# A hybrid decoder step: the first stage's loads, norm row, page table and key copies rearranged, decays stored by chunks

## The chip, the cores and the metric

The kernel runs on one core of a Trainium2 chip. The core has TensorE (PE: matrix products and transposes into PSUM), VectorE (DVE), ScalarE (ACT), GpSimd (POOL) and SyncE (SP, which here issues nearly all DMA transfers). Each engine takes its own instructions strictly in order and waits on semaphores for the others; the transfers of all queues share 16 DMA engines. The metric is the device time of one execution in microseconds (us), the median of several runs.

## The reference

One decoder layer is applied to 512 prompt tokens with 16 learned meta tokens in front, and to 64 sample tokens (8 sequences of 8). Shapes: width 1024, 32 state-space heads of 64 with state 128, 16 attention heads over 4 key/value heads, 8 indexer heads of 64.

```python
u = rmsnorm(h, norm1_w)                      # x * rsqrt(mean(x^2)+eps) * w
z, xbc, dt_raw, q, k, v, qi, ki, wi, g_ssm, g_attn = split_in(u @ w_in)
# state-space branch: causal conv + silu on xbc, then per chunk of 128 tokens
acum  = cumsum(softplus(dt_raw + dt_bias) * -exp(a_log))
decay = exp(where(causal, acum[i] - acum[j], -inf))
y     = (cb * decay) @ (x * dt) + (cc @ h) * exp(acum)
# attention branch: indexer scores choose the keys (128 of the prompt, 256 of a sample's)
s   = sum_h relu(qi . ki) * wi               # sample keys: cache_kidx[page_table]
att = softmax(q . k[top], ...) @ v[top]
# merge, then MLP
h = h + (sigmoid(g_ssm) * (y @ w_ssm_proj) + sigmoid(g_attn) * (att @ w_attn_proj)) @ w_out
h = h + square(relu(rmsnorm(h, norm2_w) @ w_up)) @ w_down
```

Outputs are the final-normalised tokens, the new key, value and indexer rows, and the new convolution and state-space states.

## The kernel before, in words

All 592 tokens stand as columns. Products that need fp32 accuracy are done as three products of rounded parts: each operand is split into a high part (a rounded copy, made by ScalarE) and a low part (the rest, made by VectorE), and `mm3` (line 145) adds high x high, low x high and high x low over 8 slices of 128 rows, 24 matmuls for one block of 128 output columns and one half of the tokens (288 or 296 columns). `weights` (line 130) loads a 512 KB block through one of two raw buffers `wr`, and splits it into `wh` (line 122) and `wl` (line 123), three buffers each. A half's result lies in one of two PSUM buffers of the tag `w`. Other PSUM results take the tags `a` and `s`, three buffers each, which `mis()` hands out in turn.

**First stage (lines 170 to 235, pool `p0`).** SP loads the first x tile of 128 tokens, the first 532 columns of the constants (`cst`, 266 KB), `norm1_w` read once for every partition (`w1row`, 512 KB), the second and third x tile, the first weight block `w0` (indexer keys, indexer weights, time steps; two transfers), the fourth tile, and a fifth one with the 64 sample and 16 meta tokens. For each of the five tiles ScalarE squares and sums (line 202), VectorE and GpSimd make the reciprocal root (lines 154, 155), VectorE multiplies by it and by the norm row (`xn`, line 205), TensorE transposes eight slices (line 211), ScalarE writes the high part `uh` (line 213) and VectorE the low part `ul` (line 214). `xn` and the squares' scratch share a tag with two buffers. Then come the loads of a second weight block (`wq0`), of the convolution weights, of `ssm_norm_w` and of the convolution state, and their transposes (lines 221 to 234). The first half of a projection needs the first three tiles, the second half all five.

**Indexer stage (lines 288 to 500, pool `p1`).** The pool takes the place of `p0`; it is declared with the default for reused memory, by which its first instructions wait for the whole of the old pool. It loads the other constants (line 290), runs the first projection (`smT`), then the four blocks of indexer queries (`qS`: ScalarE line 321, VectorE line 322), makes the page table's row numbers (lines 330 to 340: one load, seven VectorE operations), and scores the prompt's keys (lines 344 to 360). `idx_unit` (line 379) handles two sample sequences: GpSimd gathers the indexer keys of each (`kr`, two buffers), and they are copied side by side into `kg`:

```python
pool.indirect_dma_start(out=kr, ..., in_offset=bass.IndirectOffsetOnAxis(ap=idx[:, b:b + 1], axis=0))
(act.copy if b2 else pool.tensor_copy)(kg[:, :, b2, :], kr.rearrange("p (s c) -> p s c", s=8))
```

Transposes (line 394) and a product with the sample queries (line 404) follow. Then VectorE picks the top 128 keys of each prompt row (lines 420, 421). The time steps and their sums `acum` are made (lines 426 to 467); their transposed form `acT` (32 heads x 640 tokens) goes to DRAM as `d_ac`, its exponential as `d_ec` (lines 469, 471). Projections for keys, values and queries follow.

**Scan (lines 612 to 816).** Four groups of 8 heads, each with five chunks (four of 128 tokens, one of the 80 others, of which 64 are used here). For each chunk, `chunk` loads the heads' sums spread over the tokens' partitions (`bc`, two loads of four heads, line 719) and the exponentials spread over 64 partitions for each head (`EB`, two loads, line 713). ScalarE turns `bc` into decays (lines 721, 723). Convolution and gate projections are interleaved with it.

After that come gates, sample attention, prompt attention, the merge and the MLP, which the change doesn't touch.

**What sets the order.** The program is written in one order; at build time a planner goes through it with modelled times of its own, and writes each engine's instructions in the order in which they become ready in that model, earlier program lines first. On the chip this order is fixed: an instruction whose input is late holds everything behind it on its engine.

Of the kernel before, what the change touches and what calls it, by code (L numbers as in the profile page):

```python
# [33 lines left out]
def _consts():  # L34
    p = np.arange(128)[:, None]
    j = np.arange(128)[None, :]
    blk = np.where(np.arange(128) < 64, np.arange(128) // 8, np.arange(128) // 16 + 4)
    same = blk[:, None] == blk[None, :]
    v = (p // 64) * 8 + p % 8
    parts = [  # L40
        ("ident", p == j),
        ("tri", j >= p),
        ("tri4", (j >= p) & same),
        ("ones", np.ones((128, 128))),
        ("off8", np.arange(8)[None, :] != 2 * (p // 32) + p % 32 // 8),
        ("half", np.full((128, 8), -0.5)),
        ("in32", np.arange(4)[None, :] == (p % 32) // 8),
        ("blk4", same),
        ("neg", np.where(j > p, NEG, 0.0)),
        ("cneg", np.where(j > p, -BIG, 0.0)),  # L50
        ("sel", np.arange(32)[None, :] == v),
        ("neg8", np.where(np.arange(8)[None, :] > p % 8, NEG, 0.0)),
        ("in8", np.arange(8)[None, :] == p // 8),
        ("pg8", np.arange(8)[None, :] == p // 16),
        ("mod16", p % 16),
        ("odd2", (p % 2) == (j // 64)),
        ("pair16", np.arange(16)[None, :] == p // 2),
    ]
# [12 lines left out]
def body(ctx, tc, a, o):  # L71
# [36 lines left out]
    def flat(t):  # L108
        return t.rearrange("p a b -> p (a b)")
# [63 lines left out]
    p0_stack = ctx.enter_context(ExitStack())  # L173
    p0 = p0_stack.enter_context(tc.tile_pool(name="p0", bufs=1))

# [5 lines left out]

    wrow = p0.tile([128, D], FT, name="w1row")
    xts = []
    for t in range(5):
        xt = p0.tile([128, D], FT, tag="xt", name="xt", bufs=5)
        load_x(t, xt)
        if t == 4:
            sy.dma_start(xt[64:80], meta)
        if t == 2:
            w0 = weights([(lambda r: r[:, :, 0:96], w_in[:, C_KI:C_KI + 96].rearrange("(k p) c -> p k c", p=128)),  # L190
                          (lambda r: r[:, :, 96:128], w_in[:, C_DT:C_DT + 32].rearrange("(k p) c -> p k c", p=128))], lo_eng=dve)
        if t == 0:
            sy.dma_start(cst[0], a["cst"][:, 0:KEPT])
            sy.dma_start(wrow, rows(a["norm1_w"], D))
        xts.append(xt)
    ssq = p0.tile([128, 5], FT, name="ssq1")
    rs = p0.tile([128, 5], FT, name="rs1")
    for t in range(5):
        n = 128 if t < 4 else 80
        xt = xts[t]  # L200
        jk = p0.tile([128, D], FT, tag="jk", name="jk", bufs=2)
        act.activation(jk[:n], xt[:n], AF.Square, accum_out=ssq[:n, t:t + 1])
        rstd_of(rs[:n, t:t + 1], ssq[:n, t:t + 1], D, 1, n)
        xn = p0.tile([128, D], FT, tag="jk", name="xn", bufs=2)
        dve.scalar_tensor_tensor(xn[:n], xt[:n], rs[:n, t:t + 1], wrow[:n], op0=OP.mult, op1=OP.mult)
        for q in range(2):
# [5 lines left out]
            h_ = uh[:, 4 * q:4 * q + 4, 128 * t:128 * t + n]  # L212
            act.activation(h_, pv[:, :, :n], AF.Copy)
            dve.tensor_tensor(ul[:, 4 * q:4 * q + 4, 128 * t:128 * t + n], pv[:, :, :n], h_.bitcast(FT), op=OP.subtract)  # L214
    wq0 = weights([(lambda r: r, block(w_in, 0, C_QI))])

    cwr = p0.tile([128, 128], FT, name="cwr")
    sy.dma_start(cwr[0:96], a["conv_w"][0].rearrange("k (t c) -> (k t) c", c=128))
# [3 lines left out]
    act.activation(cwT, ps[:, :120], AF.Copy, scale=0.5)  # L222
    nwr = p0.tile([16, 128], FT, name="nwr")
# [4 lines left out]
    scr = p0.tile([24, 3072], FT, name="scr")  # L228
    sy.dma_start(scr, a["state_conv"][0].rearrange("b r c -> (b r) c"))
# [18 lines left out]
    d_y = drp.tile([16, 128, NQ], FT, name="d_y")  # L248
    d_ac = drp.tile([32, 640], FT, name="d_ac")
    d_ec = drp.tile([32, 640], FT, name="d_ec")  # L250
    d_xd = drp.tile([16, 128, NT], FT, name="d_xd")
# [35 lines left out]

    with tc.tile_pool(name="p1", bufs=1) as p1:
        cst.append(p1.tile([128, CST.shape[1] - KEPT], FT, name="cst1"))
        sy.dma_start(cst[1], a["cst"][:, KEPT:])  # L290
        sm_tok = p1.tile([128, 5, 128], FT, name="sm_tok")
        smT = p1.tile([128, NT], FT, name="smT")
# [34 lines left out]
        split(kiT[:, 0:528], kS, kL)  # L327


        pt = p1.tile([128, 64], I32, name="pt")  # L330
        ptf = p1.tile([128, 8, 8], FT, name="ptf")
        ptx = p1.tile([128, 8], FT, name="ptx")
        sy.dma_start(pt, rows(a["page_table"], 64))
        dve.tensor_copy(flat(ptf), pt)
        dve.tensor_tensor(ptf, ptf, K("pg8")[:, None, :].to_broadcast([128, 8, 8]), op=OP.mult)
        dve.tensor_reduce(ptx, ptf, axis=AX, op=OP.add)
        dve.tensor_scalar(ptx, ptx, 16.0, K("mod16"), op0=OP.mult, op1=OP.add)
        dve.tensor_copy(idx, ptx)
        for h in range(2):
            dve.tensor_scalar(idx2[:, :, h], ptx, 2.0, float(h), op0=OP.mult, op1=OP.add)  # L340

# [37 lines left out]
        def idx_unit(pr):  # L379
            kiP = p1.tile([128, 1032], FT, tag="kiP", name="kiP", bufs=2)  # L380
            kg = p1.tile([128, 8, 2, 64], FT, tag="kg", name="kg", bufs=2)
            for b2 in range(2):
# [3 lines left out]
                                        in_offset=bass.IndirectOffsetOnAxis(ap=idx[:, b:b + 1], axis=0))  # L386
                (act.copy if b2 else pool.tensor_copy)(kg[:, :, b2, :], kr.rearrange("p (s c) -> p s c", s=8))
            dv = kiP[:, 0:1024].rearrange("c (p s) -> c s p", s=8)
# [36 lines left out]

        brow = p1.tile([128, 2, 32], FT, name="brow")
        sy.dma_start(brow[:, 0, :], rows(a["dt_bias"], 32))
        sy.dma_start(brow[:, 1, :], rows(a["a_log"], 32))
        X = p1.tile([128, 5, 32], FT, name="X")
# [38 lines left out]
        dve.tensor_copy(acT[:, 512:640], ps[:32, 0:128])  # L468
        sy.dma_start(d_ac, acT)
        act.activation(acT, acT, AF.Exp)  # L470
        sy.dma_start(d_ec, acT)
        ps = mis()
# [139 lines left out]
    with tc.tile_pool(name="p3", bufs=1, reuse_waits="tile") as p3, \  # L612
# [88 lines left out]
        def chunk(g, c):  # L701
# [563 lines left out]
```

## Time and profile before

| | |
|---|---|
| median of 3 runs | 1494.07 us (1493.74 to 1494.7) |
| the profiled execution | 1499.61 us, its span 1497.8 us |
| busy share of the span | PE 96%, DVE 65%, ACT 46%, POOL 22% |
| mean granted clock of TensorE | 0.955 |
| DMA | 221.54 MB in 297609 packets |
| sizes of transfers | `w1row` 512 KB, `cst` 266.0 KB and 292.5 KB, `scr` 288.0 KB, x tiles and weight blocks 512 KB, `bc` 256 KB (32 times) and 64 KB (8 times), `EB` 128 KB (32 times) and 64 KB (8 times) |

A row of the timeline has the start in us, the duration, the engine, the line and the operation, its output and inputs with their shapes, how many were merged into the row, and in brackets how long the engine had been idle and what released it. The chain is the work that ended last, followed back from the end of the stretch: each step names what released the next. A wait row reads: who waited for whom, total us, times, longest. In the table by stretches, each engine's busy us stand with the number of its instructions in parentheses, then the granted clock as a share of full speed, the share of the 16 DMA engines, and GB/s. Merged matmuls overlap in the pipeline, so the duration of one is longer than the step to the next.

### The profile page before, as it was taken

To read this page: it belongs to the slowest core of one execution; us is meant where nothing else is said; L and a number is where in the kernel's file an instruction comes from. 1 tells how busy PE (TensorE), PEld (TensorE's weight loads), DVE (VectorE), ACT (ScalarE), POOL (GpSimd) and SP (SyncE) were. 2 spreads that over 40 slices of the span, in tenths; PEclk is the share of its full clock that TensorE was granted. 3 is DMA by queue.
4 is the path that set the end of the run, shared out by engine and by line. 5 is a ranking of instruction groups with operands and counts; after the bars stand their busy time and mean duration, and the time that the engine had idled before them with its cause. 6 is when DMAs were issued, how large, how long until landed. Compare 5 with 4: busy or idle time off the path is not lost.

```text
span 1497.8 us, 26553 instructions
## 1 busy us (share of the span) xinstructions
PE 1443.2 (96%) x9960; PEld 1293.7 (86%) x9960; DVE 973.9 (65%) x2010; ACT 695.1 (46%) x1548; POOL 324.1 (22%) x475
## 2 busy tenths in 40 slices
PE   6899999999999999999999999999999999999998
PEld 5899989987888888889688888898898998899886
DVE  5599989998868767582644777665654444444434
ACT  4454255546665654542655777732352331232211
POOL 1100011426636335342423633100000000000001
PEclk9899999999999999999999999999999999999999
DMA  6334365768897887878964532146143321231202
GB/s 178 107 66 118 115 173 167 208 195 220 231 263 201 255 221 197 247 198 252 293 228 142 155 87 79 43 129 194 50 133 93 99 85 57 85 112 58 84 28 70
DMA packets 297609, 221.54 MB, mean 148 GB/s; under 512 B 43821, under 2 KB 267361, under 8 KB 297457
## 3 DMA queue, kind: packets, MB, share of 16 engines
q1 hardware_dynamic: 292232, 200.98, 47.5%
q0 software_dynamic: 5248, 18.88, 3.7%
q8 instruction: 78, 1.28, 0.4%
q14 instruction: 51, 0.41, 0.1%
HBM read 174.97 MB, written 44.07 MB: 146 GB/s over the span
## 4 chain that ended last, share of the span: by engine, by line
PE 76%; DMA 11%; DVE 5%; ACT 2%; issue 2%; SPq 1%; POOL 1%; POOLq 0%; DVEq 0%; ACTq 0%
PE w L145 22%; PE s L1177 16%; PE a L145 14%; PE w L1039 7%; PE s L871 2%; PE a L1177 2%; PE s L1005 2%; DMA out_dram<-st 1%; DMA bc<-d_ac 1%; DMA wr<-in_w_ssm_proj_dram 1%; DMA st<-in_state_ssm_dram 1%; PE s L734 1%; PE a L894 1%; PE a L995 1%; DMA d_x<-tk 1%
## 5 line engine op out<-in xcount | busy, mean ns | idle before, releaser
L145 PE MATMUL w<-uh,wh 128*128 128x288 f32 (+1 forms) x1168 | 359.1, 307 | 12.8 <-DVE qS L322 4.3
L145 PE MATMUL w<-uh,wl 128*128 128x288 f32 (+1 forms) x1168 | 354.9, 304 | 0.0
L145 PE MATMUL w<-ul,wh 128*128 128x288 f32 (+1 forms) x1168 | 352.6, 302 | 0.6 <-DVE ul L214 0.6
L145 PEld LDWEIGHTS w<-uh,wh 128*128 128x128 f32 x1168 | 223.6, 191 | 20.5 <-issue 7.1
L123 DVE TENSOR_TENSOR wl<-wr,wh 128x1024 fp32r<-128x1024 f32 x129 | 161.1, 1249 | 117.1 <-ACT wh L122 114.9
L145 PEld LDWEIGHTS w<-ul,wh 128*128 128x128 f32 x1168 | 223.5, 191 | 3.9 <-issue 2.3
L145 PEld LDWEIGHTS w<-uh,wl 128*128 128x128 f32 x1168 | 222.4, 190 | 1.5 <-issue 0.8
L122 ACT ACTIVATE wh<-wr 128x1024 fp32r<-128x1024 f32 x129 | 136.3, 1056 | 147.5 <-PE w L145 84.5
L145 PE MATMUL a<-u2h,wh 128*128 128x288 f32 (+2 forms) x512 | 151.4, 296 | 0.0
L145 PE MATMUL a<-u2l,wh 128*128 128x288 f32 (+2 forms) x512 | 151.2, 295 | 0.0
L145 PE MATMUL a<-u2h,wl 128*128 128x288 f32 (+2 forms) x512 | 151.2, 295 | 0.0
L1177 PE MATMUL s<-dl,hh 128*128 128x512 f32 (+1 forms) x324 | 126.9, 392 | 0.0
L1177 PE MATMUL s<-dh,hh 128*128 128x512 f32 (+1 forms) x324 | 126.8, 392 | 0.0
L1179 DVE TENSOR_TENSOR h<-h,s 128x512 f32<-128x512 f32 (+1 forms) x91 | 61.2, 679 | 100.4 <-PE s L1177 100.3
L122 ACT ACTIVATE dh<-wr 128x1024 fp32r<-128x1024 f32 x40 | 42.5, 1062 | 178.1 <-PE s L1177 138.3
L155 POOL TENSOR_TENSOR rs<-rs,cst 128x1 f32<-128x1 f32 (+2 forms) x15 | 8.3, 552 | 446.0 <-DVE rs L154 445.9
L1177 PE MATMUL s<-dh,hl 128*128 128x512 f32 (+1 forms) x260 | 101.7, 391 | 0.0
L145 PEld LDWEIGHTS a<-u2l,wh 128*128 128x128 f32 x512 | 96.1, 188 | 0.6
L145 PEld LDWEIGHTS a<-u2h,wh 128*128 128x128 f32 x512 | 96.1, 188 | 0.6
L145 PEld LDWEIGHTS a<-u2h,wl 128*128 128x128 f32 x512 | 96.1, 188 | 0.0
L1039 PE MATMUL w<-ysh,wh 128*128 128x288 f32 x256 | 78.4, 308 | 0.2 <-DVE ms L1044 0.2
L123 DVE TENSOR_TENSOR dl<-wr,dh 128x1024 fp32r<-128x1024 f32 x40 | 49.0, 1225 | 45.3 <-ACT dh L122 45.2
(384 smaller groups left out, 3220.1 us busy)
## 6 DMA issues: line engine op xcount, KB each, us to landing
wr<-in_w_in_dram SPq DMA_DIRECT2D x64, 512.0 KB
wr<-in_w_up_dram SPq DMA_DIRECT2D x32, 512.0 KB
wr<-in_w_down_dram SPq DMA_DIRECT2D x32, 512.0 KB
st<-in_state_ssm_dram SPq DMA_DIRECT2D x16, 512.0 KB
bc<-d_ac SPq DMA_DIRECT2D x32, 256.0 KB
out_dram<-st SPq DMA_DIRECT2D x16, 512.0 KB
wr<-in_w_ssm_proj_dram SPq DMA_DIRECT2D x16, 512.0 KB
d_xd<-th SPq DMA_DIRECT2D x16, 296.0 KB
```

Of the source, the lines that this page charges most:

```text
L122: act.activation(hi, raw, AF.Copy)
L123: (lo_eng or dve).tensor_tensor(lo, raw, hi.bitcast(FT), op=OP.subtract)
L145: pe.matmul(ps[:, :c1 - c0], p[:, k, :], x[:, c0:c1], start=(k == 0 and i == 0), stop=(k == 7 and i == 2))
L155: pool.tensor_tensor(dst, dst, K("half")[:p, :cols], op=OP.pow)
L734: pe.matmul(py[64 * (hh % 2):64 * (hh % 2) + 64, 128 * (hh // 2):128 * (hh // 2) + n], xt[:n, 64 * hh:64 * hh + 64], mt, start=True, stop= ...
L871: pe.matmul(v[64 * hp:64 * hp + 64], QZ[:, hp, :], kk, start=True, stop=True)
L894: pe.matmul(py[h, 0:128], PTs[:, s, h], Vg[s // 4][:, 256 * (s % 4) + 128 * hp:256 * (s % 4) + 128 * hp + 128], start=(s == 0), stop=False)
L995: pe.transpose(pv[:, j, :], P2[:, e, 128 * j:128 * j + 128], idf)
L1005: pe.matmul(py[64 * e:64 * e + 64, 0:256], Vt[:, j, kv:kv + 64], PT[:, e, j], start=(j == 0), stop=False)
L1039: pe.matmul(ps[:, :HQ], p[:, k, mc], x[k][:, c0:c1], start=(k == 0 and i == 0), stop=(k == 3 and i == 2))
L1177: pe.matmul(ps, x, w[:, cc], start=(k == 0 and i == 0), stop=(k == len(ws) - 1 and i == len(terms) - 1))
L1179: dve.tensor_tensor(h2[:, t, cc], h2[:, t, cc], ps, op=OP.add)
```

## The change

- `norm1_w` is loaded once, as one row of 4 KB, first of all transfers. TensorE spreads it: a column of ones (one row deep, so K = 1) times the row, in two halves of 512 columns into PSUM; ScalarE copies each half to `w1row`.
- The constants are loaded in two parts. The first, 136 columns (identity and the -0.5 used as an exponent, which moved up), comes behind the first x tile, the others behind the second weight block.
- The squares' scratch has one buffer of its own, `xn` three.
- `p0` lies on the other side of the memory, its tiles are declared in front, and `p1` waits tile by tile for what lay at a tile's place.
- The page table's load and its seven operations, and the loads of the two bias rows, stand ahead of the first projection.
- GpSimd makes both copies into `kg`.
- `d_ac` is laid out as chunk, head, token; `d_ec` as chunk, parity of the head, head pair, token, and is stored by two transfers. The loads of `bc` and `EB` take whole rows of 128 tokens, in the short chunk too, so a partition's piece is 2 KB in one run.

```diff
-    p0 = p0_stack.enter_context(tc.tile_pool(name="p0", bufs=1))
+    p0 = p0_stack.enter_context(tc.tile_pool(name="p0", bufs=1, side="right"))
+    NF = CONSTS["half"][1]
+    w1r = p0.tile([1, D], FT, name="w1r")
+    one = p0.tile([1, 128], FT, name="one")
+    dve.memset(one, 1.0)
...
-        if t == 0:
-            sy.dma_start(cst[0], a["cst"][:, 0:KEPT])
-            sy.dma_start(wrow, rows(a["norm1_w"], D))
...
+    sy.dma_start(w1r, a["norm1_w"])
+    load_x(0, xts[0])
+    sy.dma_start(cst[0][:, 0:NF], a["cst"][:, 0:NF])
+    load_x(1, xts[1])
+    load_x(2, xts[2])
+    w0 = weights([(lambda r: r[:, :, 0:96], w_in[:, C_KI:C_KI + 96].rearrange("(k p) c -> p k c", p=128)),
+                  (lambda r: r[:, :, 96:128], w_in[:, C_DT:C_DT + 32].rearrange("(k p) c -> p k c", p=128))], lo_eng=dve)
+    load_x(3, xts[3])
+    load_x(4, xts[4])
+    sy.dma_start(xts[4][64:80], meta)
+    for c in range(2):
+        ps = mis()
+        pe.matmul(ps, one, w1r[:, 512 * c:512 * c + 512], start=True, stop=True)
+        act.copy(wrow[:, 512 * c:512 * c + 512], ps)
...
-        jk = p0.tile([128, D], FT, tag="jk", name="jk", bufs=2)
+        jk = p0.tile([128, D], FT, tag="jk", name="jk", bufs=1)
...
-        xn = p0.tile([128, D], FT, tag="jk", name="xn", bufs=2)
+        xn = p0.tile([128, D], FT, tag="xn", name="xn", bufs=3)
...
     wq0 = weights([(lambda r: r, block(w_in, 0, C_QI))])
+    sy.dma_start(cst[0][:, NF:], a["cst"][:, NF:KEPT])
...
-    with tc.tile_pool(name="p1", bufs=1) as p1:
+    with tc.tile_pool(name="p1", bufs=1, reuse_waits="tile") as p1:
         cst.append(p1.tile([128, CST.shape[1] - KEPT], FT, name="cst1"))
         sy.dma_start(cst[1], a["cst"][:, KEPT:])
+        pt = p1.tile([128, 64], I32, name="pt")
+        sy.dma_start(pt, rows(a["page_table"], 64))
+        brow = p1.tile([128, 2, 32], FT, name="brow")
+        sy.dma_start(brow[:, 0, :], rows(a["dt_bias"], 32))
+        sy.dma_start(brow[:, 1, :], rows(a["a_log"], 32))
+        ptf = p1.tile([128, 8, 8], FT, name="ptf")
+        ptx = p1.tile([128, 8], FT, name="ptx")
+        dve.tensor_copy(flat(ptf), pt)
+        dve.tensor_tensor(ptf, ptf, K("pg8")[:, None, :].to_broadcast([128, 8, 8]), op=OP.mult)
+        dve.tensor_reduce(ptx, ptf, axis=AX, op=OP.add)
+        dve.tensor_scalar(ptx, ptx, 16.0, K("mod16"), op0=OP.mult, op1=OP.add)
+        dve.tensor_copy(idx, ptx)
+        for h in range(2):
+            dve.tensor_scalar(idx2[:, :, h], ptx, 2.0, float(h), op0=OP.mult, op1=OP.add)
...
-                (act.copy if b2 else pool.tensor_copy)(kg[:, :, b2, :], kr.rearrange("p (s c) -> p s c", s=8))
+                pool.tensor_copy(kg[:, :, b2, :], kr.rearrange("p (s c) -> p s c", s=8))
...
-        sy.dma_start(d_ac, acT)
+        sy.dma_start(d_ac.rearrange("c h n -> h c n"), acT.rearrange("h (c n) -> h c n", c=5))
...
-        sy.dma_start(d_ec, acT)
+        for e in range(2):
+            sy.dma_start(d_ec[:, e].rearrange("c i n -> i c n"), acT.rearrange("(i e) (c n) -> e i c n", e=2, c=5)[e])
...
-                src = d_ec[g8, 128 * c:128 * c + n].rearrange("(i e) n -> e i n", e=2)[e]
-                sy.dma_start(EB[64 * e:64 * e + 64, :, :n], src[None].to_broadcast([64, 4, n]))
+                sy.dma_start(EB[64 * e:64 * e + 64], d_ec[c, e, None, g4].to_broadcast([64, 4, 128]))
...
-                sy.dma_start(bc[:n, :, :n], d_ac[None, h0:h0 + 4, 128 * c:128 * c + n].to_broadcast([n, 4, n]))
+                sy.dma_start(bc[:n], d_ac[c, None, h0:h0 + 4].to_broadcast([n, 4, 128]))
```

## Rows read from the trace of the kernel before

**Rows 1.** The page, busy us of TensorE, its share, instructions.

```profile
PE 1443.2 (96%) x9960; PEld 1293.7 (86%) x9960; DVE 973.9 (65%) x2010; ACT 695.1 (46%) x1548; POOL 324.1 (22%) x475
```

**Rows 2.** Busy us by stretch: PE, PEld, DVE, ACT, POOL; clock, DMA share, GB/s.

```profile
0.00:60.00 60.00, 39.85 (x247) 37.45 (x247) 34.63 (x72) 26.42 (x54) 11.51 (x18) 0.89 0.61 160
60.00:200.00 140.00, 139.35 (x996) 130.97 (x997) 128.91 (x317) 62.11 (x142) 7.55 (x14) 0.95 0.39 102
200.00:800.00 600.00, 574.53 (x4409) 509.99 (x4407) 433.59 (x786) 327.14 (x769) 229.21 (x269) 0.94 0.77 221
```

**Rows 3.** Waits of the first 60 us: total, times, longest.

```profile
PE s L211 <- DVE xn L205: 13.6, 4, 9.5
...
ACT kg L387 <- DMA kr<-in_cache_kidx_dram,idx: 7.2, 2, 5.5
...
PE w L145 <- DVE qS L322: 4.3, 1, 4.3
```

**Rows 4.** The chain of the first 50 us: start, us, what.

```profile
9.52 1.13 PE s L211 x4
...
31.24 3.40 DMA dsr<-in_d_skip_dram
...
43.44 0.62 ACT kg L387
```

**Rows 5.** The timeline of the first 30 us.

```profile
4.21 1.06 ACT L202 ACTIVATE jk<-xt 128x1024 f32<-128x1024 f32 x1 [2.20 <-DMA xt<-in_x_prompt_dram]
...
8.18 1.28 DVE L205 SCALAR_TENSOR_TENSOR xn<-xt,rs,w1row 128x1024 f32<-128x1024 f32 x1 [2.63 <-DMA w1row<-in_norm_w_dram]
9.41 1.06 ACT L202 ACTIVATE jk<-xt 128x1024 f32<-128x1024 f32 x1 [4.04 <-DMA xt<-in_x_prompt_dram]
...
19.94 1.06 ACT L122 ACTIVATE wh<-wr 128x1024 fp32r<-128x1024 f32 x1 [2.34 <-DMA wr<-in_w_in_dram]
...
27.27 0.43 ACT L213 ACTIVATE uh<-a 128x320 fp32r<-128x320 f32 x1
...
28.88 0.40 PE L145 MATMUL w<-uh,wh 128*128 128x296 f32 x1
```

**Rows 6.** DMA of the first 15 us: packets, MB, share of 16 engines.

```profile
q1 hardware_dynamic: 3287, 3.86, 88.5%
```

**Rows 7.** The chain of the first 420 us.

```profile
104.81 0.59 PE a L394 x4
...
110.80 1.92 PE a L404 x6
```

**Rows 8.** ScalarE's groups, first 28 us: busy us, mean ns, idle before.

```profile
L202 ACT ACTIVATE jk<-xt 128x1024 f32<-128x1024 f32 (+1 forms) x5 | 5.3, 1051 | 6.2 <-DMA xt<-in_x_prompt_dram 6.2
L122 ACT ACTIVATE wh<-wr 128x1024 fp32r<-128x1024 f32 x3 | 3.2, 1055 | 2.6 <-DMA wr<-in_w_in_dram 2.6
L213 ACT ACTIVATE uh<-s 128x512 fp32r<-128x512 f32 (+1 forms) x5 | 2.8, 561 | 2.7 <-PE s L211 2.4
```

**Rows 9.** The chain from 30 to 80 us.

```profile
45.11 5.52 PE w L145 x24
...
52.62 6.69 PE w L145 x48
```

**Rows 10.** Busy us by stretch, 45 to 50 us.

```profile
45.00:50.00 5.00, 4.89 (x21) 4.92 (x22) 4.29 (x8) 2.95 (x6) 2.73 (x4) 0.52 0.38 113
```

**Rows 11.** Instructions of line 387: ns min/median/max, first and last start.

```profile
L387 POOL COPY kg<-kr x4: 610/898/1397, 39.0 to 119.0; 128x512 f32<-128x512 f32 x4
```

**Rows 12.** DMA from 200 to 800 us: packets, MB, share.

```profile
q1 hardware_dynamic: 183699, 115.96, 69.1%
```

**Rows 13.** All waits from 200 to 800 us.

```profile
ACT bc L721 <- DMA bc<-d_ac: 38.6, 23, 4.7
```

**Rows 14.** TensorE's waits from 200 to 420 us.

```profile
PE a L771 <- POOL xd L767: 3.1, 1, 3.1
PE w L145 <- ACT rb L566: 2.6, 2, 1.7
```

More of the change, by code (lines that the diff above doesn't have):

```diff
@@ L41, in _consts @@
         ("ident", p == j),
+        ("half", np.full((128, 8), -0.5)),
         ("tri", j >= p),
@@ L45, in _consts @@
         ("off8", np.arange(8)[None, :] != 2 * (p // 32) + p % 32 // 8),
-        ("half", np.full((128, 8), -0.5)),
         ("in32", np.arange(4)[None, :] == (p % 32) // 8),
@@ L173, in body @@
     p0_stack = ctx.enter_context(ExitStack())
-    p0 = p0_stack.enter_context(tc.tile_pool(name="p0", bufs=1))
+    p0 = p0_stack.enter_context(tc.tile_pool(name="p0", bufs=1, side="right"))
+    NF = CONSTS["half"][1]
+    xts = [p0.tile([128, D], FT, tag="xt", name="xt", bufs=5) for _ in range(5)]
+    w1r = p0.tile([1, D], FT, name="w1r")
+    one = p0.tile([1, 128], FT, name="one")
+    dve.memset(one, 1.0)
+    wrow = p0.tile([128, D], FT, name="w1row")
+    ssq = p0.tile([128, 5], FT, name="ssq1")
+    rs = p0.tile([128, 5], FT, name="rs1")
+    cwr = p0.tile([128, 128], FT, name="cwr")
+    nwr = p0.tile([16, 128], FT, name="nwr")
+    scr = p0.tile([24, 3072], FT, name="scr")
     def load_x(t, dst):
@@ L180, in load_x @@
             sy.dma_start(dst[0:64], xs)
[L182 to L191, printed above, removed]
-        if t == 0:
-            sy.dma_start(cst[0], a["cst"][:, 0:KEPT])
-            sy.dma_start(wrow, rows(a["norm1_w"], D))
-        xts.append(xt)
-    ssq = p0.tile([128, 5], FT, name="ssq1")
-    rs = p0.tile([128, 5], FT, name="rs1")
+    sy.dma_start(w1r, a["norm1_w"])
[12 more added lines that the diff above has]
+        act.copy(wrow[:, 512 * c:512 * c + 512], ps)
     for t in range(5):
@@ L212, in body @@
             h_ = uh[:, 4 * q:4 * q + 4, 128 * t:128 * t + n]
-            act.activation(h_, pv[:, :, :n], AF.Copy)
-            dve.tensor_tensor(ul[:, 4 * q:4 * q + 4, 128 * t:128 * t + n], pv[:, :, :n], h_.bitcast(FT), op=OP.subtract)
+            ch = act.activation(h_, pv[:, :, :n], AF.Copy)
+            cl = dve.tensor_tensor(ul[:, 4 * q:4 * q + 4, 128 * t:128 * t + n], pv[:, :, :n], h_.bitcast(FT), op=OP.subtract)
     wq0 = weights([(lambda r: r, block(w_in, 0, C_QI))])
-    cwr = p0.tile([128, 128], FT, name="cwr")
+    sy.dma_start(cst[0][:, NF:], a["cst"][:, NF:KEPT])
     sy.dma_start(cwr[0:96], a["conv_w"][0].rearrange("k (t c) -> (k t) c", c=128))
@@ L222, in body @@
     act.activation(cwT, ps[:, :120], AF.Copy, scale=0.5)
-    nwr = p0.tile([16, 128], FT, name="nwr")
     sy.dma_start(nwr, a["ssm_norm_w"][0].rearrange("(t c) -> t c", c=128))
@@ L227, in body @@
     act.copy(nwT, ps[:, :16])
-    scr = p0.tile([24, 3072], FT, name="scr")
     sy.dma_start(scr, a["state_conv"][0].rearrange("b r c -> (b r) c"))
@@ L248, in body @@
     d_y = drp.tile([16, 128, NQ], FT, name="d_y")
-    d_ac = drp.tile([32, 640], FT, name="d_ac")
-    d_ec = drp.tile([32, 640], FT, name="d_ec")
+    d_ac = drp.tile([5, 32, 128], FT, name="d_ac")
+    d_ec = drp.tile([5, 2, 16, 128], FT, name="d_ec")
     d_xd = drp.tile([16, 128, NT], FT, name="d_xd")
@@ L327, in body @@
         split(kiT[:, 0:528], kS, kL)
[L330 to L340, printed above, removed]
         wis = p1.tile([128, 4, 8], FT, name="wis")
@@ L423, in body @@
             dve.tensor_tensor(at[:, LT[t] - 128:], at[:, LT[t] - 128:], K("cneg"), op=OP.min)
-        brow = p1.tile([128, 2, 32], FT, name="brow")
-        sy.dma_start(brow[:, 0, :], rows(a["dt_bias"], 32))
-        sy.dma_start(brow[:, 1, :], rows(a["a_log"], 32))
         X = p1.tile([128, 5, 32], FT, name="X")
```

## The prediction

> **What bounds it now.** I read the page first: TensorE is busy for 1443.2 us [rows 1] of the span of 1497.8. The 54.6 us of idle time, and stretches at its lower clock, are all that a change can win that leaves the matmuls alone. The windows say where it lies [rows 2]: 20.15 us in the first 60, 0.65 in the next 140, 25.5 between 200 and 800, some 8 after that. From 60 to 200 TensorE is full and VectorE has 128.91 of 140; nothing is to be had there, but both get their work from the first 60 us, so an earlier start there should move the rest as a block. The waits of the first 60 us [rows 3] name two: TensorE stands 13.6 for the normalised rows, ScalarE 7.2 for gathered index keys. The chain and the timeline of that stretch [rows 4, 5] give the moments used below. The profiled execution took 1499.61, its span and 1.81 around it; the runs' median is 1494.07. I work out differences in the profiled execution and take them off the median.
>
> **Loads and norm row.** Ahead of the second x tile the queue now carries the norm row for all partitions (512 KB) and the first constants (266 KB). The change puts 4 KB and 68 KB there (136 columns x 4 B x 128 partitions): 706 KB less, 0.72 MB. The first 15 us move 3.86 MB [rows 6], 0.257 MB per us: 2.8 us. So the second tile's square can start at 6.6 instead of 9.41 [rows 5], and what follows it lands up to 2.8 earlier. The rest of the constants goes behind the second weight block; nothing in the x tiles' path needs it.
>
> The row is now spread by two K=1 products; no row shows one. Its 4 KB load: 0.1 KB took 3.40 from issue to landing [rows 4], so 0.73 + 3.40 = 4.1; as the other bound I take half of that latency, 2.4. The product: 1032 fp32 columns took 1.92 [rows 7], 0.95 for 512. Four transposes at that place took 0.59 [rows 7], the kernel's first four 1.13 [rows 4], so at the start all goes at half that speed, 1.9 each, 3.8 for two. The second copy from PSUM adds 0.56 (a `uh` copy, 2.8/5 [rows 8]). Row ready: 4.1 + 3.8 + 0.56 = 8.5 at the slow end, 2.4 + 1.9 + 0.56 = 4.9 at the fast end. Now the first xn starts at 8.18 after 2.63 of waiting [rows 5], so at best it gains 2.6. If the two copies stand ahead of the first square on ScalarE, it loses some 2. I take the slow end, 0.3 later: no gain here by itself.
>
> What counts is the end of the stage. The second half of the first projection starts at 28.88 [rows 5], since it needs all five x tiles, and 1.18 after the last `uh` copy ends (27.27 + 0.43). Before that lies ScalarE's list. From the first square, at 4.21 [rows 5], it holds five squares 5.3, three weight roundings 3.2, ten `uh` copies (two rows like the one shown) 5.6 [rows 8], and now two row copies 1.1: 15.2, so it ends at 19.4 if it never waits. It waited 2.34 for the second weight block [rows 5]; I keep that: 21.7, the half at 22.9, 6.0 earlier. VectorE's links and TensorE's slow transposes between ScalarE's steps are not on the list, so I take 4.0, between 0 (a late transfer holds ScalarE as long as now) and 7. What is late next: ScalarE itself. Three xn buffers of their own and one for the squares change nothing: no row shows an xn waiting for its buffer, and squares follow each other on one engine.
>
> **Index keys on GpSimd.** The largest term. ScalarE's copy of a gather waited 5.5 us [rows 3], to 43.44 [rows 4]; behind it in ScalarE's queue stood the `qS` copies that free TensorE's two w buffers, so TensorE stood 4.3 [rows 3] until 45.11. It resumed slowly: 24 products took 5.52, where 48 took 6.69 right after [rows 9], so 3.35 would do: 2.17 lost. The granted clock of 45 to 50 is 0.52 [rows 10], the 1.2 GHz level, behind an engine that had stood idle. Then 1.99 pass until 52.62 [rows 9], with few score products in them, for ScalarE is still late with `qS`; I count 1.5 as lost. Sum 4.3 + 2.17 + 1.5 = 8.0. I take 7.0, since the exchange of `qS` with VectorE will keep part of the last term; bounds 3 (only a shorter stall) and 9 (all, and gaps after it). GpSimd gets four copies more. Its own four took 0.61 to 1.40, median 0.90 [rows 11], ScalarE's 0.62 [rows 4]. Behind a copy that waits on GpSimd stand the next gathers, whose user, the transposes of the keys, first run at 104.81 [rows 7], 50 us later: 0, unless the reciprocal roots of the last x tiles stand behind it (rival b).
>
> The row shows GpSimd's copies stretched from 0.61 to 1.40. The Trainium skill ("SBUF — State Buffer", Who interferes with whom) says that a VectorE instruction with two SBUF inputs and a GpSimd one that reads SBUF lock each other out for a whole instruction. That speaks against these copies: by it, four more hold VectorE up to 4 x 0.61 = 2.4 us in its full stretch, and the sum would give 1485.5. No row shows VectorE losing it, so it is not counted.
>
> **Page table, buffers one by one.** Constants, page table and bias rows needn't wait for the end of the first stage any more. Their four issues on SP come ahead of later weight blocks, whose raw buffer isn't free yet: 0. ScalarE no longer waits for a bias row, but the projection kept TensorE busy over that wait: 0. The page table's seven VectorE operations move ahead; if VectorE comes to them before the table has landed, the xn rows stand behind them. The table has 512 + 198 + 288 + 292 KB ahead of it in the queue, 1.32 MB, 5.1 us at 0.257, so it lands 5 after the last x tile, whose xn is due 2 after: price up to 3, inside the 0 to 7 above.
>
> **Decays by chunks.** 40 loads of `bc` and 40 of `EB` read 512 B pieces (256 B in the short chunk): 32 x 512 + 32 x 256 + 8 x 512 = 28,672. They become 32 x 128 + 8 x 64 + 40 x 64 = 7,168 of 2 KB, and the short chunk's whole rows add 1.05 MB. If packets set the cost, 21,504 of 183,699 go, 11.7% [rows 12]; if bytes do, 1.05 comes on top of 115.96 MB, 0.9%. The first 15 us cost 16 x 15 x 0.885 / 3.86 = 55 us of an engine per MB at 1.17 KB a packet [rows 6], this stretch 16 x 600 x 0.691 / 115.96 = 57 at 0.63 KB [rows 12]: bytes. ScalarE waits 38.6 for `bc` [rows 13], but TensorE's waits on ScalarE there are small, 2.6 the largest [rows 14]. By packets 11.7% of 25.5 idle is 3.0 won; by bytes 0.2 lost. I take 0. The stores in their new shape lie in the full stretch, long before they are read: 0.
>
> **Sum.** 4.0 + 7.0 + 0 = 11.0: 1488.6 profiled, 1483.1 in the median.
>
> **Rivals.** (a) All of it is won: 7 + 9 + 3 = 19, 1475. For: 20 us of idle stand there. Against: the first products stay at the low speed.
> (b) Only the index-key stall goes, while VectorE or GpSimd, in order, stands at the page table or a gathered key ahead of the last x tiles: 7 - 2 = 5, 1489. For: ScalarE stood 5.5 at just such a wait, so the order laid down beforehand trusts transfers too much. Against: the table lands only shortly after the last tile.
> (c) The change doesn't do what it says: ScalarE is held at the same place by another wait and the first stage ends as late: within 3 of 1494.
> (d) Slower: between 200 and 800 the engines' orders are laid out anew from the earlier start, and TensorE, in order, gets more waits like its 3.1 for GpSimd's squares [rows 14]. It decides from 11 us on, against 25.5 idle there now. One more such wait in each of the four groups is 12.4, 1495.5; two are 24.8, 1507.9; I put it at 1502. For: 25.5 us show that this order is tight. Against: nothing in it is made longer but eight short loads.
>
> **How the numbers follow.** Forecast (8 to 15 won) 0.45, (a) 0.18, (b) 0.17, (c) 0.07, (d) 0.13. 0.2% is 3.0 us, about what a measurement of this kernel can tell from no change: faster 0.80, same 0.07, slower 0.13. The forecast's own range is 1479 to 1486. The range for 8 in 10 takes in (b), (c) and most of (a), and leaves out the far end of (a), 0.07, and (d), 0.13: 1472 to 1495.
>
> **What would show it.** The second half of the first projection starts near 25 (right) or after 28 (wrong), the second square near 6.6. No ScalarE wait for gathered keys; from there to the first key projection, which begins 11 earlier than now, no TensorE gap over 1 us and a granted clock near 0.95. Idle time from 200 to 800 stays at 22 to 28. The prediction is wrong if that grows by 11, or if VectorE stands over 4 us for the page table before the fifth xn.

## The result, and the profile after

| | before | after |
|---|---|---|
| median of 12 runs each, taken together | 1493.07 us (1487.39 to 1499.17) | 1486.47 us (1480.00 to 1491.02) |
| ratio, 95% interval | | 0.995 (0.9931 to 0.9968) |
| the same kernel in a later comparison (27 and 12 runs) | 1493.98 us | 1489.70 us, 0.9966 (0.9946 to 0.9986) |
| the profiled execution | 1499.61 us | 1491.02 us |

It is faster, by 6.6 us and by 4.3 in the two comparisons; the forecast was 11.0. One kernel's runs lie 11 us apart, so a term of 2 us doesn't show in a median of 12. Most readings below are moments inside the first 73 us, in several profiles.

The page and the windows of the changed kernel answer [rows 1, 2]: busy us of PE, PEld, DVE, ACT, POOL, then clock, DMA share, GB/s.

```profile
PE 1440.7 (97%) x9964; PEld 1293.0 (87%) x9964; DVE 975.5 (66%) x2011; ACT 693.8 (47%) x1546; POOL 327.7 (22%) x479
...
0.00:60.00 60.00, 47.85 (x294) 43.45 (x295) 37.08 (x76) 27.68 (x58) 13.14 (x20) 0.91 0.61 159
60.00:200.00 140.00, 138.14 (x990) 129.84 (x990) 130.56 (x316) 63.61 (x150) 8.47 (x16) 1.00 0.43 111
200.00:800.00 600.00, 574.13 (x4439) 510.80 (x4438) 432.80 (x791) 324.44 (x759) 233.17 (x272) 0.99 0.76 220
```

TensorE's idle time in the first 60 us went from 20.15 to 12.15. From 200 to 800 it stands at 25.9 against 25.5: what was won at the start was not given back there. The first key projection begins at 66.69 instead of 72.47, 5.8 earlier. Not all of that is the change's, for this execution of the kernel before started late: its first indexer query projection starts at 33.85, while e1, e12 and e7 below, which keep its first stage, have 31.38, 30.62 and 31.41. Part of the difference is a stretch at a granted clock of 0.50, the 1.2 GHz level, which none of those three has in that half of the first projection:

```profile
30.00:32.00 2.00, 2.00 (x10) 2.00 (x9) 0.00 (x0) 0.00 (x0) 0.00 (x0) 0.50 0.59 156
```

So one moment of one profile says little here. Better measures are the mean of several profiles, or the distance from the query to the key projection within one.

The timeline of the changed kernel's first stage answers [rows 5]; columns as there.

```profile
2.25 2.04 PE L207 MATMUL s<-w1r,one 1*128 1x512 f32 x2 [2.25 <-DMA w1r<-in_norm_w_dram]
4.09 1.91 PE L207 MATMUL a<-w1r,one 1*128 1x512 f32 x2
7.03 1.06 ACT L213 ACTIVATE jk<-xt 128x1024 f32<-128x1024 f32 x1 [0.83 <-DMA xt<-in_x_prompt_dram]
8.76 2.48 DVE L216 SCALAR_TENSOR_TENSOR xn<-xt,rs,w1row 128x1024 f32<-128x1024 f32 x2 [0.39 <-ACT w1row L208]
15.70 1.04 ACT L213 ACTIVATE jk<-xt 80x1024 f32<-80x1024 f32 x1
21.60 1.06 ACT L122 ACTIVATE wh<-wr 128x1024 fp32r<-128x1024 f32 x1 [2.85 <-DMA wr<-in_w_in_dram]
26.16 0.40 PE L145 MATMUL w<-uh,wh 128*128 128x296 f32 x1
```

The second square starts at 7.03 (forecast 6.6), the first xn at 8.76 (8.5), the second half at 26.16 (25). Each of these moments is near its forecast; what they are worth is another matter, below.

The chain of waits, first of the kernel before from 20 to 46 us, then of the changed one in its first 80 (start, us, what):

```profile
27.45 0.75 PE s L233 x12
28.20 0.76 PE a L233 x12
28.98 0.35 SPq L290
29.38 0.88 SPq L333
...
31.24 3.40 DMA dsr<-in_d_skip_dram
...
36.75 6.67 DMA kr<-in_cache_kidx_dram,idx
```

```profile
23.95 0.37 SPq L130
24.36 0.57 SPq L299
24.99 0.43 SPq L301
25.46 0.43 SPq L303
25.94 4.62 DMA brow<-in_a_log_dram
30.77 1.05 ACT wh L122
31.85 1.23 DVE wl L123
33.15 0.36 DVE kiT L319
33.59 5.35 DMA kiT<-kiT
38.96 0.65 ACT kS L122
...
44.48 9.06 PE w L145 x48
54.30 3.46 PE w L145 x24
```

Read the two from their ends. Before, ScalarE was let go at 43.44 by a gather; now at 38.96 by another transfer, the one (line 320) that doubles the key rows `kiT` to the second 64 partitions. That is 4.5 of the 5.8 between these two profiles. Both chains come from a string of small loads on SP (constants, page table, bias rows, D row). Before, it began when the last transposes of the first stage had ended (line 233, 28.96); now at 24.36, right behind a weight block.

The new wait still costs. TensorE stands 2.69 us, then works at 0.50 to 0.52 of its clock, the 1.2 GHz level, and its next 48 products take 9.06 where [rows 9] has 6.69. These two rows are the timeline and the windows (columns as above):

```profile
43.54 0.49 PE L363 MATMUL s<-kS,qS 128*128 128x144 f32 x1 [2.69 <-DVE qS L345]
...
45.00:50.00 5.00, 5.00 (x23) 5.00 (x22) 3.94 (x12) 0.00 (x0) 2.78 (x4) 0.52 0.36 102
```

### The profile page after: what moved, and what is told of

Its sections match the earlier page's. It is cut to its first block, busy times and chain, and to the rows that moved or that the text cites. A ratio compares the mean times of both kernels' runs of the same rounds, so it can differ in the third digit from the quotient of the medians.

```text
span 1489.2 us, 26558 instructions
## 1 busy us (share of the span) xinstructions
PE 1440.7 (97%) x9964; PEld 1293.0 (87%) x9964; DVE 975.5 (66%) x2011; ACT 693.8 (47%) x1546; POOL 327.7 (22%) x479
## 4 chain that ended last, share of the span: by engine, by line
PE 81%; DMA 8%; DVE 5%; ACT 2%; SPq 2%; POOL 1%; issue 1%; POOLq 0%; DVEq 0%; ACTq 0%
PE w L145 25%; PE s L1184 16%; PE a L145 14%; PE w L1046 7%; PE s L1012 2%; PE a L1184 2%; PE s L878 2%; PE s L741 1%; DMA xt<-d_x 1%; PE a L1002 1%; DMA bc<-d_ac 1%; PE a L901 1%; PE s L753 1%; PE s L870 1%; DVE wl L123 1%
## 5 line engine op out<-in xcount | busy, mean ns | idle before, releaser
L123 DVE TENSOR_TENSOR wl<-wr,wh 128x1024 fp32r<-128x1024 f32 x129 | 164.2, 1273 | 110.0 <-ACT wh L122 99.6
```

Of the source, the lines that this page charges most:

```text
L123: (lo_eng or dve).tensor_tensor(lo, raw, hi.bitcast(FT), op=OP.subtract)
```

## Experiments on the index keys

**One edit alone: both gathered-key copies on GpSimd, all else as before** (e1).

```diff
-(act.copy if b2 else pool.tensor_copy)(kg[:, :, b2, :], ...)
+pool.tensor_copy(kg[:, :, b2, :], ...)
```

> The kernel before with one edit: GpSimd makes both copies of the gathered keys. TensorE's, VectorE's and SP's orders stay as they were. Theory A (the stall was worth its length, but ScalarE's next instruction, the rounding of the indexer keys, waits for the transfer that doubles them, which lands some 5.4 us after its issue at 37.5): the 4.3 us gap before the second query block goes, a new gap of 2 to 3 us stands before that block's second half, with a slow stretch behind it; the key projection starts 3 to 4.5 us before 72.5, and the time is 1489 to 1490. Theory B (the first stage's loads carry all of the gain, a wait of ScalarE only changes its name): the key projection starts within 1 us of 72.5, time within 1.5 us of before. Theory C (my forecast's term): 7 us earlier, 1486.

Measured: 1493.78, ratio 0.999 (0.9971 to 1.001). ScalarE's waits from 28 to 68 us (who waited for whom: total, times, longest):

```profile
ACT kS L122 <- DMA kiT<-kiT: 4.0, 1, 4.0
```

It is let go at 42.86 instead of 43.44, and query and key projection are 38.65 apart, as before (38.62). The largest term of the forecast, alone, is worth nothing: the rounding of the doubled keys stands next in ScalarE's queue, and its transfer is as late as the gather was.

**The other wait alone** (e12): the doubled rows are made by VectorE.

```diff
-        sy.dma_start(kiT[64:128], kiT[0:64])
+        dve.tensor_copy(kiT[64:128, 0:16], smT[0:64, 576:592]); dve.tensor_copy(kiT[64:128, 16:592], smT[0:64, 0:576])
```

> The kernel before with the doubled key rows made by VectorE alone; ScalarE still copies every second gather. Theory B2 (two late transfers in a row, each alone worth nothing): ScalarE waits 4 or more for gathered keys, the first query projection and the key projection 38 to 39 apart, median within 1.5 of the kernel before. Rival K (the doubling transfer alone is the limit): 36 or less apart, median 2.5 or more below the kernel before.

Measured: 1492.71, ratio 1.0006 (0.9991 to 1.0021). ScalarE waits for gathered keys again, now with nothing ahead of it:

```profile
ACT kg L387 <- DMA kr<-in_cache_kidx_dram,idx: 5.1, 2, 2.8
```

Query and key projection are 37.2 apart where 38 to 39 was expected: a little was won, and the run's median shows none of it.

**Both** (e7, both diffs on the kernel before).

> The kernel before with two things done to the index keys alone: GpSimd makes both copies of gathered keys, and the doubled key rows are made by two VectorE copies instead of a transfer. Theory B2 (ScalarE stands at the first of two late transfers, so only both together free it; the gathered keys alone gave 0): no ScalarE wait over 1 us from the first query projection to the key projection, these two 32 to 34 apart instead of 38.6, no half-speed stretch between them, median 4.5 to 6 below the kernel before. Rival B3 (the first stage's late start makes a third wait there, for the page table that comes late): apart 36 or more, median within 2 of the kernel before.

Measured: 1490.31, ratio 0.9966 (0.9946 to 0.9987), 3.7 below the kernel before where 4.5 to 6 was expected. The longest wait of ScalarE behind these transfers is 1.7, for VectorE's `qS`. The projections are 33.5 apart instead of 38.6, and the next products run at full pace (23 in 3.35). Two late transfers in a row, each worth nothing in the median alone, make 5 us together between the two projections.

**The changed kernel with the copy back on ScalarE** (e2, the first diff reversed).

> The changed kernel with one edit undone: ScalarE again makes every second copy of the gathered keys. The orders of TensorE, VectorE and SP stay as in the changed kernel. Theory A: the second gather lands near 39.7, so ScalarE stands there some 3 to 4 us and TensorE stands about 4 us at about 36.5; the key projection starts 1 to 2.5 us later than in the changed kernel (66.7), near 68.5; the time lies 1 to 2.5 us above it. Theory B: the same start within 0.5 us. Theory C: 7 us later, no gain left over the kernel before but for the loads' 4.

Measured: 1488.18, ratio 0.9962 (0.9945 to 0.9979). ScalarE waits for the gather:

```profile
ACT kg L397 <- DMA kr<-in_cache_kidx_dram,idx: 6.1, 1, 6.1
```

It is let go at 41.21, against 38.96 in the changed kernel. Query and key projection are 39.16 apart, against 37.02, 36.86 and 37.30 in three profiles with that copy on GpSimd (after, e5, e4): on top of the rest the move is worth some 2 us there. The medians (1488.18 against 1486.47 and 1489.70) don't tell it.

**The changed kernel without the doubling transfer**, twice (e3, e8; the diff of e12).

> The changed kernel, but the indexer keys are doubled into the upper 64 partitions by two VectorE copies instead of a transfer. Theory A (this transfer is what took the gain back): ScalarE's wait of 3.0 us for it is gone, TensorE's gap of 2.7 us before the second query block's second half too, and the slow 48 products (9.1 us against 6.7) run at full speed; the key projection starts near 61.7 instead of 66.7, and the time is 5 us under the changed kernel, 1481 to 1482. Rival D (VectorE's exchange with ScalarE over the queries is late anyway): the start moves by under 1.5 us, and the gap stands there with another name.

> The changed kernel with the doubled key rows made by two VectorE copies instead of a transfer, now beside the changed kernel in the same call. Theory B2: the first query projection and the key projection 32 to 33 apart (37.0 in the changed kernel), median 1482.5 to 1484.5, 3 to 4.7 below the changed kernel. Rival R (what is won at the start is given back where the orders from 200 to 800 are laid out anew): the key projection as early, but the median within 1.5 of the changed kernel's.

Measured: 1483.12, ratio 0.9935 (0.991 to 0.996), and 1483.55, ratio 0.9922 (0.9896 to 0.9948), each over 6 runs; in the second comparison the changed kernel stood at 1489.70 beside it. The projections are 32.3 and 32.0 apart instead of 37.0. This version beats the kernel before, and by its medians the changed one too (6.2 in that comparison; the two intervals just overlap). Of e8's first stage, the windows:

```profile
0.00:60.00 60.00, 47.80 (x321) 43.82 (x322) 40.05 (x84) 29.01 (x63) 14.44 (x20) 0.97 0.60 165
```

PE is as busy as in the changed kernel, but at a granted clock of 0.97 instead of 0.91 it gets through 321 products instead of 294.

## Experiments on the first stage

**The changed kernel again, and with its first loads as before** (e5, e6).

```diff
-    sy.dma_start(w1r, a["norm1_w"])
     load_x(0, xts[0])
-    sy.dma_start(cst[0][:, 0:NF], a["cst"][:, 0:NF])
+    sy.dma_start(cst[0], a["cst"][:, 0:KEPT])
+    sy.dma_start(wrow, rows(a["norm1_w"], D))
...
-    for c in range(2):
-        ps = mis()
-        pe.matmul(ps, one, w1r[:, 512 * c:512 * c + 512], start=True, stop=True)
-        act.copy(wrow[:, 512 * c:512 * c + 512], ps)
```

> The changed kernel itself, run again beside the next three so that they can be set against it. Theory A (the early start is worth some 6 us and is carried through): 1486 to 1488, ratio to the kernel before 0.995 to 0.997; the first indexer query projection starts at 29.7 to 31.0, the key projection 36.5 to 37.5 later, at 66.5 to 68. Theory D (the start gained in the first profile was one lucky execution): the first query projection starts at 32 or later, ratio above 0.997.

> The changed kernel with its first loads as before: norm row read once for every partition, all first constants in one transfer behind the first x tile; buffers, page table, key copies and decays stay changed. Theory L4 (the term as forecast, 4.0): second square at 9.3, second half of the first projection at 30 to 31, first query projection at 34, median 4 above the changed kernel in the same call. Theory L2 (the term is about half, as the starts of five profiles so far suggest): half at 28.5 to 29.5, query projection at 32 to 33, median 1.5 to 2.5 above. Theory L0 (the earlier start comes from the page table and the buffers' waits, not from the loads): half within 0.7 of the changed kernel's, median within 0.7.

Measured: 1489.70, 0.9966 (0.9946 to 0.9986), and 1487.74, 0.9952 (0.9932 to 0.9973). e5's median lies 1.7 above what was expected, its starts do as expected: first query projection 30.01, key projection 66.87. With the old loads they are 29.77 and 65.97, no later. The second square waits as in [rows 5], yet the fifth starts at 17.58 and not at 21.38:

```profile
9.95 1.06 ACT L213 ACTIVATE jk<-xt 128x1024 f32<-128x1024 f32 x1 [4.69 <-DMA xt<-in_x_prompt_dram]
...
17.58 1.05 ACT L213 ACTIVATE jk<-xt 80x1024 f32<-80x1024 f32 x1
```

So the new loads and the norm row's product bring nothing that is left at the stage's end; the theory that fits is L0, though the median, 2.0 below e5's, leaves its 0.7 on the fast side. (Its half starts at 24.32, but only one product of it; the convolution state's 24 transposes stand behind that one, so the start of the half is no measure there.)

**One edit alone: buffers of their own for xn, all else as before** (e9).

```diff
-        jk = p0.tile([128, D], FT, tag="jk", name="jk", bufs=2)
+        jk = p0.tile([128, D], FT, tag="jk", name="jk", bufs=1)
-        xn = p0.tile([128, D], FT, tag="jk", name="xn", bufs=2)
+        xn = p0.tile([128, D], FT, tag="xn", name="xn", bufs=3)
```

> The kernel before with one edit: the scratch of the squares has one buffer and the normalised rows three of their own, as in the changed kernel; loads, pool, page table, key copies and decays stay. Theory O (this edit is what brings the first stage forward: with shared buffers the order laid down puts the fifth square behind the second weight block's rounding, which waits for its transfer; with buffers of their own it stands ahead of it): the fifth square starts at 17 to 18 instead of 21.38, the last xn at 21 to 22.5 instead of 25.01, the first query projection at 29.5 to 30.5, with the loads of before. The stall for gathered keys stays, so the median is 0 to 2.5 below the kernel before. Rival P (the pool that waits tile by tile and the early page table bring it): the first query projection at 31.4 or later.

Measured: 1490.85, ratio 0.999 (0.9975 to 1.0004). The fifth square starts at 17.25 and the last xn at 21.24. With shared buffers they start at 21.38 and 25.01 before, and at 18.90 to 19.75 and 23.24 to 24.04 in e1, e12 and e7; against the mean of the four (23.89) the last xn is 2.6 earlier. The query projection starts at 30.65 (expected 29.5 to 30.5), 1.2 ahead of the mean of the four (31.82), but e12 has 30.62 with shared buffers, so this start alone shows nothing. The key projection starts at 67.46. The chain:

```profile
25.07 0.76 PE a L233 x12
25.88 0.35 SPq L290
26.28 0.42 SPq L333
...
33.37 5.79 DMA kr<-in_cache_kidx_dram,idx
39.17 0.62 ACT kg L387
```

The transposes that SP waits for end earlier, and the small loads begin 3.1 ahead of the kernel before, 2.2 ahead of the mean of the four (28.04). ScalarE is let go 4.3 ahead of the kernel before, but only 1.2 ahead of e12 (40.34), where the gather is also the last to land.

**The changed kernel with that edit undone** (e10).

> The changed kernel with that one edit undone: squares and normalised rows share two buffers again; the norm row is still spread by products and the loads are the new ones. Theory O: the fifth square stands behind the second weight block's rounding again, the first query projection starts at 31.5 to 34, 1.5 or more after the changed kernel's 29.67 and 30.01, median 1 to 4 above the changed kernel's 1486.5 to 1489.7. Rival P, or the loads after all: the first query projection at 30.8 or earlier.

Measured: 1485.11 over 7 runs, ratio 0.9953 (0.9936 to 0.997): not 1 to 4 above the changed kernel. The fifth square stands behind the weight rounding again (18.22), and the query projection starts at 31.76, both as expected; but the key projection starts at 64.95, earlier than in the changed kernel. The chain and the wait of TensorE:

```profile
24.97 0.61 ACT uh L224
...
28.45 3.21 PE w L145 x22
31.68 1.07 ACT wh L122
...
34.53 5.12 DMA kiT<-kiT
39.68 0.65 ACT kS L122
...
45.13 6.68 PE w L145 x48
```

Its small loads start at 23.89 and are no part of this chain; the first projection is. In the changed kernel that projection is over 2.1 earlier and the chain runs over the bias row instead, so the release comes only 0.7 earlier; the rest is spent standing. Here TensorE stands 1.85 instead of 2.69 and isn't slow afterwards (6.68 for 48; the granted clock from 45 to 50 is 1.00, against 0.52), which gives the rest back.

**Three edits: e7 with buffers of their own** (e11): no new loads, no norm row product, old page table, flat decays.

> The kernel before with own buffers for the normalised rows, both gathered-key copies on GpSimd, and the doubled key rows made by VectorE: no new loads, no norm row product, old page table, flat decays. Theory O with B2: the first query projection at 29.5 to 30.5 and the key projection 32 to 34 later, at 62 to 64.5, as early as in the changed kernel without the doubling transfer (62.26 and 63.86); median 1482.5 to 1487. Rival P: the key projection at 65 or later, median above 1488.

Measured: 1486.59 over 6 runs, ratio 0.9948 (0.9927 to 0.9969); query projection 30.27, key projection 64.31. Two small edits of the change, and one that isn't in it, do about as much as the whole change, by the medians.

**Side by side.** From each profile's timeline and chain: when SP issues the first small load (`cst1`), when the query projection starts, when ScalarE starts what waited for the last late transfer, which transfer, and when the key projection starts.

| | small loads | query projection | let go | by | key projection |
|---|---|---|---|---|---|
| before | 28.98 | 33.85 | 43.44 | gather | 72.47 |
| e1 | 27.97 | 31.38 | 42.86 | doubling | 70.03 |
| e12 | 27.21 | 30.62 | 40.34 | gather | 67.81 |
| e9 | 25.88 | 30.65 | 39.17 | gather | 67.46 |
| e2 | 25.63 | 30.98 | 41.21 | gather | 70.14 |
| after, e5 | 24.36, 23.53 | 29.67, 30.01 | 38.96, 39.15 | doubling | 66.69, 66.87 |
| e4 | 24.89 | 30.54 | 40.31 | doubling | 67.84 |
| e6 | 24.68 | 29.77 | 39.00 | doubling | 65.97 |
| e10 | 23.89 | 31.76 | 39.68 | doubling | 64.95 |
| e7, e11, e3, e8 | 28.01, 27.03, 24.87, 23.82 | 31.41, 30.27, 31.53, 30.24 | not held | | 64.87, 64.31, 63.86, 62.26 |

The key projection follows the release by 25.3 to 29.0: the release sets most of it, the pace behind it the rest. The four profiles with the kernel before's first stage (before, e1, e12, e7) issue the small loads at 28.0 on average, the eight with the changed pool (after, e5, e4, e2, e6, e10, e3, e8) at 24.5. Starts of one and the same first stage lie up to 3.2 apart, so the means count: the query projection starts at 31.8 in those four and at 30.5 in the six with the whole new first stage (after, e5, e4, e2, e3, e8). From there to the key projection it is 38.6 in the kernel before and 37.1 in the changed one (after, e5, e4). Together the key projection is some 3 us earlier, not 5.8.

## Experiment on the decays

**The changed kernel with the flat layout** (e4; `d_ec` and the loads of `EB` go back likewise).

```diff
-    d_ac = drp.tile([5, 32, 128], FT, name="d_ac")
+    d_ac = drp.tile([32, 640], FT, name="d_ac")
...
-            sy.dma_start(bc[:n], d_ac[c, None, h0:h0 + 4].to_broadcast([n, 4, 128]))
+            sy.dma_start(bc[:n, :, :n], d_ac[None, h0:h0 + 4, 128 * c:128 * c + n].to_broadcast([n, 4, n]))
```

> The changed kernel with the decays' layout undone (heads by 640 tokens, loads of 512 B pieces). Theory A (bytes set the cost, nothing on TensorE's path waits for these loads): the key projection starts at the same 66.7, TensorE's idle time from 200 to 800 stays within 2 us of the changed kernel's 25.9, time within 2 us. Rival E (packets set the cost): idle time there up by 3 us or more, and ScalarE's waits for the loads of the sums up by a tenth or more.

Measured: 1491.0, ratio 0.9971 (0.9951 to 0.9992), beside 0.995 and 0.9966 with chunks: not told apart. From 200 to 800 us the queue of the changed kernel moves (packets, MB, share of 16 engines) the first row; the wait of ScalarE for `bc` is the second row there and the third in e4:

```profile
q1 hardware_dynamic: 161680, 115.54, 67.8%
```

```profile
ACT bc L728 <- DMA bc<-d_ac: 36.6, 21, 3.8
```

```profile
ACT bc L728 <- DMA bc<-d_ac: 41.3, 21, 3.5
```

22,019 packets fewer than in [rows 12] for about the same MB, and the share goes from 69.1 to 67.8%: bytes set most of it. ScalarE's wait is some 5 us shorter in sum, and of the 14 profiles the seven with chunks have 33.4 to 43.4 of it (mean 37.1), the seven flat ones 38.6 to 45.1 (42.0). Through the scan, from the 500th to the 3500th product of `mm3`, the seven with chunks take 575.3 to 583.2 (mean 580.1), the flat ones 580.5 to 590.8 (584.2). A gain of up to 4 us may lie there, but six of the flat ones differ from the others in more than the layout, and e4 takes 582.4 against 581.7 and 583.2 in the changed kernel. TensorE's idle time from 200 to 800 is 27.3 in e4 against 25.9 and 25.0 (after, e5), within the 2 us of theory A; ScalarE's wait, up by more than a tenth, is what rival E named. It stays open.

Something behind the start does differ. The key projection of e2 starts as late as that of e1 (70.14 and 70.03), yet in the same comparison its median lies 5.6 lower (1488.18 and 1493.78), and its profile is 5.2 shorter behind that moment, 3.7 of it through the scan (580.8 and 584.5). The layout is only one of the edits in which these two differ.

## Why the prediction was right, and where it was wrong

The time came out inside the range and 3.4 us above the forecast (6.6 in the later comparison). The view behind it held in part: idle time at the start can be won (e7, e3, e8), but the start is some 3 us earlier where the medians differ by 6.6 and 4.3, and e1 beside e2 shows that a part lies behind it. That the sum came out as near as it did is luck in good part: its 4.0 measured nothing, its 7.0 some 2, and what did more was put at 0.

- **Loads and norm row, 4.0.** The transfers did as worked out, and two K=1 products took 3.75, as priced (3.8), though their row landed at 2.25 instead of 4.1: the second copy stands behind the second square, so the row is ready at 8.66 (8.5). The step that failed is the next one, that earlier squares shorten the stage. With the old loads the stage ends as early (e6).
- **Buffers "change nothing".** Wrong. I looked for an xn that waits for its buffer; no row shows one, because the order laid down had already put the fifth square behind a weight block's transfer. With buffers of their own it stands ahead of it, and the last xn comes 2.6 earlier than the mean of the four profiles without (e9). Taking them back in the changed kernel costs nothing that the time shows (e10).
- **Page table, constants and bias rows: 0.** This is the term that was priced wrongest. I argued that SP's queue would hold them behind weight blocks anyway, and that TensorE has work over ScalarE's wait for a bias row. Both are true in the changed kernel: that wait lasts 5.17 where it was 5.04. But it ends 3.86 earlier (30.64 against 34.50), and the issue of the doubling transfer, two steps behind it, comes 3.87 earlier (33.59 against 37.46). Off TensorE's path at that moment, it was on the path of what ScalarE waits for next. The release begins here. On the mean, ScalarE's instruction on the bias row starts at 33.59 in the four profiles of the old first stage and at 30.91 in the eight with the changed pool, 2.7 earlier. In the old pool the small loads are held by the end of the first stage, so an earlier end does nearly the same: the doubling transfer is issued at 34.08 with the buffers alone (e9), at 34.53 with the changed pool and shared buffers (e10), at 33.59 to 34.67 with both. The pool's declaration alone was not tried.
- **Index keys on GpSimd, 7.0.** Alone 0 (e1), on top of the rest about 2 from query to key projection (e2). The missing look was at ScalarE's next instruction: its transfer was issued 0.7 after the gather [rows 4 has the copy; 37.46 against 36.75], and landed as late (42.84 in e1). Rival (c), held at the same place by another wait, came true in part, and the low clock, counted at 2.17, is still there behind the new wait (9.06 - 6.69 = 2.37).
- **GpSimd's copies, 0.** Held on the whole. The rule of the Trainium skill ("SBUF — State Buffer", Who interferes with whom) that spoke against them can be seen in the timelines, first of VectorE and GpSimd after, then of the operation of line 446 before:

```profile
39.64 0.71 DVE L123 TENSOR_TENSOR kL<-kiT,kS 128x528 fp32r<-128x528 f32 x1 [2.20 <-ACT kS L122]
40.27 0.73 DVE L446 TENSOR_TENSOR s__1173<-e__1170,w__1174 128x160 f32<-128x160 f32 x1
...
98.34 0.74 DVE L369 SCALAR_TENSOR_TENSOR am<-ri,wis,am 128x528 f32<-128x528 f32 x1
...
100.36 1.19 DVE L369 SCALAR_TENSOR_TENSOR am<-ri,wis,am 128x528 f32<-128x528 f32 x1
...
39.74 1.08 POOL L397 COPY kg<-kr 128x512 f32<-128x512 f32 x1 [0.59 <-DMA kr<-in_cache_kidx_dram,idx]
```

```profile
47.16 0.31 DVE L439 TENSOR_TENSOR s__1163<-e__1160,w__1164 128x160 f32<-128x160 f32 x1
```

  The copy starts while `kL`, which has two inputs, is under way, and takes 0.47 longer than the copies' median of 0.61; the two-input operation that starts inside the copy takes 0.42 longer. Beside two more copies, from 100.39, the one at 100.36 takes 0.45 longer than its like at 98.34. The trace agrees with the rule. These two cost VectorE 0.9 of the bound of 2.4; whether any of it reached the time, no run here shows.
- **Decays, 0.** Not refuted; the bound by packets, 3.0, is as possible.
- **Rival (d)**, orders between 200 and 800 laid out anew and worse: no. Idle 25.9 against 25.5.

What the gain consists of, then, as far as the runs show it: small loads that start earlier let the doubling transfer be issued some 3 us earlier (34.0 on the mean of after, e5, e4, e2 and e6, 37.0 of before and e1), and the copy's move to GpSimd makes that transfer, not the gather, the one that counts. Neither has the size or the place that was forecast. What the medians show beyond the 3 us of the start stays open; the decays are one candidate.

## What to carry to other kernels

When an instruction waits for a late transfer, look at what stands behind it on its engine and when that one's data lands; the price of the wait is only what lies between the two. Small loads in front of an address computation belong to the path of whatever is gathered, however idle they look, and a pool that waits as a whole can hold them. A buffer that no instruction is seen to wait for can still set the order, if the order was laid down for it. And before a start is compared between two profiles, look how far it moves between profiles in which nothing ahead of it was changed: here it was 3.2 us, as much as the effect.

## What was not expected of the hardware

- The granted clock of 60 to 200 us is 0.95 before [rows 2] and 1.00 after, and 24 products take 3.46 in both (the chain at 60.06 before, the row at 54.30 above). Shares of 0.94 to 0.95 change no pace here. At 0.50 (before, 30 to 32 us) products of 296 columns follow each other by 0.245, against 0.135 from 23 to 24 us of the same profile, at 0.95.
- The doubling transfer, 148 KB from SBUF to SBUF, took 5.35, 5.12 and 6.40 from issue to landing (after, e10, e1), while other loads shared the engines; the two VectorE copies that replace it left no wait over 0.2.
